# The delta layer's z weights split in two parts, and a gate row of the attention layer made late: one Trainium2 core

## The chip, the cores and the metric

The kernel runs on one core of one Trainium2 chip, as one program that is launched once. The metric is the device time of a run in microseconds (us). Three runs of the kernel before gave 1406.49, 1402.58 and 1404.82, a median of 1404.82; the execution that was profiled took 1404.2, its span on the core, from the first to the last instruction, 1402.4. Engines are called by the profile's names: PE (TensorE, the matmuls), PEld (its weight loads), DVE (VectorE), ACT (ScalarE), POOL (GpSimd), SP (the queue that issues the weight transfers).

## What is computed

Three layers follow each other on one sequence of 256 tokens of width 1024, all in float32. Cut to what matters here:

```
cond = silu(c)
for i in range(2):                                    # i = 0: delta rule, i = 1: forgetting attention
    mod = cond @ ada_w[i] + ada_b[i]                  # 3 x 1024
    shift, scale, gate = split(mod, 3)
    h = rmsnorm(x, norm_w[i]) * (1 + scale) + shift
    y = gdn_mixer(h, ...) if i == 0 else fox_mixer(h, ...)
    x = x + gate * y
x = rmsnorm(x, final_norm_w)

def gdn_mixer(h):   # q, k: 1024, v: 2048, z: 2048 columns of h @ w_in
    o = gated_delta_rule(conv_silu(q, k, v), ...)     # in chunks, by inverses of triangular matrices
    return (rmsnorm(o) * silu(z)) @ w_out
def fox_mixer(h):   # q, k, v, z of h @ w_in, and f, 16 columns
    cum = cumsum(log_sigmoid(f + f_bias))             # decides the logits of every head
    return (attention(q, k, v, cum) * silu(z)) @ w_out
```

The third layer (sliding-window attention, pooling, and 256 gathers of expert rows for each of 16 block-head pairs) isn't touched.

## The kernel before

**Weights.** All weights of the layers stand in a list of units, `plan` (from L271). A unit is 512 KB: 128 partitions by 4 blocks of 256 columns. `load` (L303) issues a unit's transfer on SP into one of 4 buffers named `raw`. `cast` (L311) then makes two tiles of it: `hi` on ACT (L329), the weight rounded to the fp32r format, and `lo` on DVE (L330), what the rounding left; `hi` and `lo` have 4 buffers each. `unit` (L339) hands the next one to PE and casts up to 3 ahead. With the two parts, a product of float32 values is three fp32r matmuls: x's high part by `hi`, x's low part by `hi`, x's high part by `lo`. So a unit makes 24 matmuls of 256 columns (the tile `pd`).

**Whole units.** `whole` (L335) names the units that are not cast: the second half (index 1 of the third number) of every unit of `awi`, the delta layer's input weights. There `raw` itself goes to PE as float32 against the float32 activations `xw`: 8 matmuls, which the profile shows as 16 passes (`pd<-raw,xw` for z, `pd<-xw,raw` for q, k, v). `awi` has column blocks 0 to 7 for q and k, 8 to 15 for v, 16 to 23 for z.

**Modulation.** `ada` (L594) makes one 128-element column of `mod` at a time: a 512 KB transfer of ada_w into a `raw` buffer, and one DVE instruction, the dot product `jk` (L600), that reads it with `silc`, silu of c. There are 48: 16 at the start, the other 32 from a generator `trickle` that `unit` steps once for each unit from the tenth on. Columns 24 to 39 are the attention layer's shift and scale, 40 to 47 its gate. `gate_row` (L631) turns 8 gate columns into a row, `gaterow`, on all partitions: 8 matmuls of 128 columns (`ps<-const,mod`, 16 passes) and 2 ACT copies (L628).

**Order.** The program is written by small tasks (`Mix`, L158) that take turns, and a scheduler then fixes one order for each engine. Each engine's instructions stand and run in that one order. The delta layer's list is `GDN_DENSE` (L48), the attention layer's `FOX_DENSE` (L49): v0 (2 units), q0 and q1 (4 units each, for q and k), v1, z0, and so on. PSUM has 2 buffers `pd`; a finished chunk is copied out of its `pd` by ACT (for q and k: `fd` L1127 and `fsq` L1129, of which `fd` has 2 buffers, given back when PE has transposed them, `ps<-const,fd`).

**The attention layer's start.** `last_dense` (L386) ends the delta layer by token blocks and makes the attention layer's features `fm` (ACT L408, DVE L492, L493). Then `gate_row(1)` is run (L1072). The task `forget` (L1076) makes the forget gate: its weights `bf` are split into `bfh` and `bfl` on DVE, an instruction that is kept behind the last `jk` written so far (L522); PE multiplies (`ps<-fm,bfh`), ACT copies (`bfc`), PE transposes, and DVE computes softplus in a chain of some 28 small instructions (`fx`, `spf`) that ends in `dup` (L569); PE's `ps<-const,dup` sums it up, and ACT and DVE store it as `nrow`, which every head's logits need. `fox_scale` (L1094) normalises q and k on DVE (`fss`, `frs`, `fd`).

Of the kernel before, what the change touches and what calls it, by code (L numbers as in the profile page):

```python
# [210 lines left out]
def build(nc, tc, ctx, I, out, dbg=None, stop=None):  # L211
# [32 lines left out]
    def t4(name, shape=(128, 1024), dt=F32):  # L244
        return t4p.tile(list(shape), dt, name=name, tag="t4", bufs=T4)


    def row_ap(n, w):
        return bass.AP(tensor=I["row"].tensor, offset=I["row"].offset + RO[n], ap=[[0, 128], [1, w]])
# [21 lines left out]
    plan = []  # L271
# [29 lines left out]
    trickle = [iter(())]  # L301
# [32 lines left out]

    def whole(i):  # L335

        return i < len(plan) and plan[i][0] == "awi" and plan[i][2] == 1

    def unit(key, ahead=LA):  # L339
        assert plan[at["use"]] == key, (plan[at["use"]], key)  # L340
# [6 lines left out]
    A2 = (("A", 0, 0, 256, 0), ("A", 1, 0, 256, 256))  # L347
    B2 = (("B", 0, 0, 128, 0), ("B", 0, 128, 128, 256))

    def dense(n, j, items, xf, kgs=(0, 1)):  # L350

        return (yield from dense_all(n, [j], items, xf, kgs))[0]

    def dense_all(n, js, items, xf, kgs=(0, 1)):

        yield from PD.get(len(js))
        pts = [psd.tile([128, 512], F32, name="pd") for _ in js]
        for (ki, kg), (j, pt) in itertools.product(enumerate(kgs), zip(js, pts)):  # L360
            wh, wl_ = unit((n, j, kg))
            for ni, (kind, bi, c0, w, o0) in enumerate(items):
                for k in range(KU):
                    xh, xl, *xw = xf(kg * KU + k)
                    if wl_ is None:
                        xh = xw[0]
                    if kind == "A":
                        ts = slice(bi * 128, bi * 128 + 128)
                        cs = slice(c0, c0 + w)
                        prods = [(xh[:, ts], wh[:, k, cs])]  # L370
                        if wl_ is not None:
                            prods += [(xl[:, ts], wh[:, k, cs]), (xh[:, ts], wl_[:, k, cs])]
                    else:
                        w = T
                        cs = slice(c0, c0 + 128)
                        prods = [(wh[:, k, cs], xh)]
                        if wl_ is not None:
                            prods += [(wh[:, k, cs], xl), (wl_[:, k, cs], xh)]
                    for i, (l, r) in enumerate(prods):
                        mm(pt[:, o0:o0 + w], l, r, start=ki == 0 and ni == 0 and k == 0 and i == 0,  # L380
                           stop=ki == len(kgs) - 1 and ni == len(items) - 1 and k == KU - 1 and i == len(prods) - 1,
                           skip_group_check=True)
                    yield 0
        return pts
# [48 lines left out]
    def run(gen):  # L433

        out = []

        def task():
            out.append((yield from gen))

        M.spawn(0, task())  # L440
        M.run()
        return out[0]


    def ahead(task, n):

        if not n:
            yield from task
            return
        while True:  # L450
            with tc.high_priority(offset=n):
                try:
                    y = next(task)
                except StopIteration:
                    return
            yield y
# [21 lines left out]
    def squares(part, src):  # L478

        jk = act.tile([128, D], BF, name="jka", bufs=1)  # L480
        return A.activation(jk[:, :src.shape[1]], src, AF.Square, accum_out=part).ins
# [112 lines left out]
    def ada(ts):  # L594

        for t in ts:
            w = wts.tile([128, KU * CW], F32, name="raw", bufs=RAW_BUFS)
            nc.sync.dma_start(w, I["ada"][:, t, :])
            jk = act.tile([128, D], BF, name="jk", bufs=1)
            i = V.scalar_tensor_tensor(jk, w, 0.5, silc, op0=OP.mult, op1=OP.mult, accum_out=mod[:, t:t + 1])  # L600
            ada_last.append(i.ins)
            ada_done.add(t)
            yield

    def mod_cols(t, n):
        assert ada_done.issuperset(range(t, t + n))
        V.tensor_tensor(mod[:, t:t + n], mod[:, t:t + n], col("ab", 48)[:, t:t + n], op=OP.add)
        return mod[:, t:t + n]
# [11 lines left out]
    def rows_of(row, m):  # L620

        for hf in range(2):
            yield from PS.get()
            p = pss.tile([128, 512], F32, name="ps")
            for k in range(4):
                o = hf * 4 + k
                mm(p[:, k * 128:(k + 1) * 128], m[:, o:o + 1].to_broadcast([128, 128]), ident, start=True, stop=True)
            A.activation(row[:, hf * 512:hf * 512 + 512], p, AF.Copy)  # L628
            PS.put(HOP)

    def gate_row(i):  # L631
        gb = ear.tile([128, 1024], F32, name="gaterow", bufs=1)
        yield from rows_of(gb, mod_cols(24 * i + 16, 8))
        return gb

    def add_gated(pt, gate, j):

        cs = slice(j * CW, (j + 1) * CW)
        p3 = pt.rearrange("p (b c) -> p b c", b=2)
        t = ear.tile([128, 2, CW], F32, name="gt", bufs=1)  # L640
        V.tensor_tensor(t, p3, gate[:, None, cs].to_broadcast([128, 2, CW]), op=OP.mult)
        V.tensor_tensor(xs[:, :, cs], xs[:, :, cs], t, op=OP.add)

    def add_gated_block(b, jj, pt, gate):
        cs = slice(jj * 512, (jj + 1) * 512)
        t = ear.tile([128, 512], F32, name="gt", bufs=1)
        V.tensor_tensor(t, pt, gate[:, cs], op=OP.mult)
        V.tensor_tensor(xs[:, b, cs], xs[:, b, cs], t, op=OP.add)
        return xs[:, b, cs]
# [61 lines left out]
    def gates():  # L711
        yield 3 * HOP
        pba = yield from small_proj("aba", 32, hx, "aba")
        A.activation(beta, pba[:, :, 0:16], AF.Tanh, scale=0.5)
        V.tensor_scalar(beta, beta, 0.5, 0.5, op0=OP.mult, op1=OP.add)
        ax_ = gp_.tile([128, 32], F32, name="ax")
        V.tensor_tensor(ax_.rearrange("p (b h) -> p b h", b=2), pba[:, :, 16:32],
                        dtb[:, None, :].to_broadcast([128, 2, 16]), op=OP.add)
        PS.put(HOP)
        sp = softplus(ax_, 32, "spa")  # L720
        A.activation(alog, alog, AF.Exp)
        V.scalar_tensor_tensor(g_tm, sp.rearrange("p (b h) -> p b h", b=2), -1.0,
                               alog[:, None, :].to_broadcast([128, 2, 16]), op0=OP.mult, op1=OP.mult)
        yield 4 * HOP
        yield from PS.get()
        pg = pss.tile([128, 3, 16], F32, name="ps")
        mm(pg[:, 0:2], C["tri"], g_tm, start=True, stop=True)
        mm(pg[:, 2], C["cross"], g_tm[:, 0], start=True, stop=True)
        V.tensor_scalar(gsum, pg, -1.0, None, op0=OP.mult)
        PS.put(HOP)  # L730
        grow.append((yield from head_rows(g_tm, C["tri"], C["tri"], "grow")))
        ev_gates.set(HOP)
# [304 lines left out]
        for d in GDN_DENSE[:-1]:  # L1037
            yield from {"q": qk_chunk, "v": v_chunk, "z": z_chunk, "w": w_out}[d[0]](int(d[1]))

    trickle[0] = ada(range(16, 48))  # L1040
    M.spawn(0, ahead(gates(), PR_QK))
    M.spawn(0, ahead(invert(0), PR_INV))
    M.spawn(0, ahead(invert(1), PR_INV))
# [25 lines left out]
    fx = ctx.enter_context(ExitStack())  # L1069
    fp = fx.enter_context(tc.tile_pool(name="fox", bufs=1, side="right", reuse_waits="tile"))  # L1070
    hx = lambda kt, fm=fm: (fm[0][:, kt], fm[1][:, kt])
    gate1 = run(gate_row(1))  # L1072
    nrow = []
    ev_f = Event(M)

# [170 lines left out]
    xo1 = lambda kt: (ohi[:, kt], olo[:, kt])  # L1246
# [4 lines left out]
    lnm = t4("lnm")  # L1251
    nc.scalar.dma_start(lnm, row_ap("lnm", 1024))

    def fox_dense():
        for d in FOX_DENSE:
            yield from {"q": fox_qk, "v": fox_v, "z": fox_z}[d[0]](int(d[1]))
        for i in range(4):
            yield from pdone[i].wait()
        for j in range(4):
            add_gated((yield from dense("bwo", j, A2, xo1, (0,))), gate1, j)  # L1260
            PD.put(HOP)

    M.spawn(-2, ahead(forget(), PR_FS))
    M.spawn(99, fox_dense())
    M.run()
    yb, yl = {}, {}

    def fox_last(b, jj, pt):
        x = add_gated_block(b, jj, pt, gate1)
        squares(ssp[:, b, jj:jj + 1], x)  # L1270
        if jj == 0:
            yb[b] = t4("yb")
        cs = slice(jj * 512, (jj + 1) * 512)
        V.tensor_tensor(yb[b][:, cs], x, fnw[:, cs], op=OP.mult)
        i = squares(ssy[:, b, jj:jj + 1], yb[b][:, cs])
        if jj == 0:
            yl[b] = t4("yl")
        V.tensor_tensor(yl[b][:, cs], yb[b][:, cs], lnm[:, cs], op=OP.mult)
        return i
# [8 lines left out]

    fm = fm_tiles()
    end = last_dense("bwo", 1, xo1, fox_last, blk_rows, fm)  # L1290
    with tc.issue_after(end):
        ss = act.tile([128, 2], F32, name="n_sf")
# [409 lines left out]
```

## Time and profile before

| | |
|---|---|
| median of 3 runs | 1404.82 us (1402.58 to 1406.49) |
| the profiled execution | 1404.2 us, of which 1402.4 are the span |
| PE, PEld busy | 1226.8, 892.3 us |
| DVE, ACT, POOL busy | 1048.0, 571.2, 353.0 us |
| mean granted PE clock | 0.965 of full |
| delta layer | from about 50 to 372 us of the span |
| attention layer | from about 377 to 533 us |
| weight transfers on SP | 512 KB each, median 3.3 to 5.3 us from issue to landing |
| gathers of the last layer | 268.45 MB, from about 740 us to the end |

Busy times overlap. PE's are modelled: a matmul counts from its start to its end, though the next starts long before, so what PE can do is read from the distance of starts. In the chain of waits each piece stands with its start and length. A pass of a float32 matmul counts as one matmul.

### The profile page before, as it was taken

The page shows a single profiled execution, that of the slowest core. Times are in us where ns is not written, and L with a number is a line of the kernel's source. Part 1 is how long each engine was busy: PE and PEld are TensorE (multiplying, and loading weights), DVE is VectorE, ACT ScalarE, POOL GpSimd, SP SyncE. Part 2 cuts the span into 40 slices and gives each one's busy share as a digit, 9 for nine tenths or more (in the row PEclk, how much of TensorE's full clock was granted, in tenths as well). Part 3 has the DMA queues.
Part 4 walks back from the last instruction along what each step waited for, and adds up shares of the span by engine and source line. Part 5 has one row for each costly group of instructions (what it writes and reads, how often), then busy time and mean ns, then how long its engine had stood idle before and what let it go on. Part 6 is the DMA issues. An engine that isn't in the chain of part 4 may idle for free.

```text
span 1402.4 us, 20440 instructions
## 1 busy us (share of the span) xinstructions
PE 1226.8 (87%) x7068; PEld 892.3 (64%) x7068; DVE 1048.0 (75%) x2683; ACT 571.2 (41%) x1310; POOL 353.0 (25%) x295
## 2 busy tenths in 40 slices
PE   2999999999999998999989997878878878777876
PEld 1889988899899988889986753333333323333332
DVE  6799989897777688774788766676767776767655
ACT  3457756574555555564435422122223221222211
POOL 0000000000000000000013436555555455555552
PEclk9999999999999999999999999999999999999999
DMA  8555355533354434335678999999999999999995
GB/s 307 196 185 188 121 182 173 187 119 118 111 183 148 151 117 152 119 107 177 184 278 344 362 376 426 426 425 426 426 426 425 426 425 426 425 426 425 426 425 225
DMA packets 72086, 392.40 MB, mean 280 GB/s; under 512 B 8112, under 2 KB 8624, under 8 KB 39472
## 3 DMA queue, kind: packets, MB, share of 16 engines
q0 software_dynamic: 37296, 268.45, 46.2%
q1 hardware_dynamic: 33104, 117.94, 25.3%
q10 hardware_dynamic: 1584, 4.72, 0.9%
q8 instruction: 56, 0.92, 0.2%
q14 instruction: 46, 0.38, 0.1%
HBM read 390.03 MB, written 1.05 MB: 279 GB/s over the span
## 4 chain that ended last, share of the span: by engine, by line
PE 52%; DMA 34%; DVE 9%; issue 3%; ACT 2%; SPq 0%; POOL 0%; POOLq 0%; DVEq 0%; ACTq 0%
PE pd L218 29%; DMA er<-uv,idx 29%; PE pacc L218 9%; PE ps L218 7%; PE acc L218 2%; PE ip L218 2%; DVE lo L330 2%; PE ps L222 1%; DMA er<-uv,i 1%; DMA raw<-awi 1%; PE po L218 1%; DVE jk L1605 1%; DVE jk L600 1%; PE pt L222 1%; DMA xs<-x 1%
## 5 line engine op out<-in xcount | busy, mean ns | idle before, releaser
L218 PE MATMUL pacc<-er,dg 128*128 128x512 f32 x1024 | 490.4, 634 | 119.0 <-ACT dg L1615 116.1
L1602 POOL DMA_INDIRECT er<-uv,idx x253 | 330.2, 1305 | 743.2 <-DVE xs L1484 435.6
L218 PEld LDWEIGHTS pacc<-er,dg 128*128 128x128 f32 x1024 | 201.0, 202 | 393.3 <-issue 227.8
L1605 DVE SCALAR_TENSOR_TENSOR jk<-er,xn 128x1024 bf16<-128x1024 f32 x256 | 312.7, 1222 | 176.8 <-DMA er<-uv,idx 176.5
L330 DVE TENSOR_TENSOR lo<-raw,hi 128x1024 fp32r<-128x1024 f32 x138 | 168.2, 1222 | 67.6 <-ACT hi L329 67.2
L329 ACT ACTIVATE hi<-raw 128x1024 fp32r<-128x1024 f32 x138 | 146.2, 1060 | 143.3 <-PE pd L218 107.0
L218 PE MATMUL pd<-fm,hi 128*128 128x256 f32 x1008 | 199.9, 295 | 3.3 <-ACT hi L329 3.3
L1609 ACT ACTIVATE ge<-dots,r 128x4 f32<-128x4 f32 (+2 forms) x79 | 23.4, 296 | 415.7 <-DVE jk L1605 415.7
L218 PEld LDWEIGHTS pd<-fm,hi 128*128 128x128 f32 x1008 | 160.2, 193 | 9.1 <-issue 4.1
L218 PE MATMUL pd<-fm,lo 128*128 128x256 f32 x504 | 145.7, 289 | 0.0
L218 PE MATMUL pd<-hi,fm 128*128 128x256 f32 (+1 forms) x608 | 116.9, 290 | 0.6 <-DVE fm L492 0.6
L218 PEld LDWEIGHTS pd<-fm,lo 128*128 128x128 f32 x504 | 96.9, 192 | 1.7 <-issue 1.7
L218 PEld LDWEIGHTS pd<-hi,fm 128*128 128x128 f32 x608 | 95.6, 192 | 1.7 <-PE ps L218 0.8
L1615 ACT ACTIVATE dg<-const,ge 128x128 f32<-128x128 f32 x250 | 81.0, 390 | 38.2 <-DVE ge L1611 32.5
L218 PE MATMUL pd<-lo,fm 128*128 128x256 f32 (+1 forms) x304 | 86.6, 286 | 0.0
L218 PE MATMUL pd<-xw,raw 128*128 128x256 f32 x256 | 67.6, 389 | 2.5 <-DVE xw L508 2.5
L600 DVE SCALAR_TENSOR_TENSOR jk<-raw,silc 128x1024 bf16<-128x1024 f32 x48 | 58.6, 1220 | 2.6 <-DMA raw<-ada 2.2
L823 POOL TENSOR_SCALAR_AFFINE_SELECT am<-am 128x256 f32<-128x256 f32 x16 | 6.5, 406 | 209.5 <-DVE am L821 198.8
L218 PEld LDWEIGHTS pd<-lo,fm 128*128 128x128 f32 x304 | 58.0, 191 | 0.2 <-DVE lo L330 0.2
L869 ACT ACTIVATE is<-acc 128x256 f16<-128x256 f32 x96 | 36.9, 385 | 31.2 <-PE acc L218 29.4
L218 PEld LDWEIGHTS pd<-xw,raw 128*128 128x128 f32 x256 | 44.0, 190 | 6.5 <-DVE xw L508 2.8
L875 DVE TENSOR_TENSOR iy<-ip,fac 128x256 f16<-128x256 f32 x96 | 40.5, 422 | 7.3 <-PE ip L218 5.9
(393 smaller groups left out, 2102.1 us busy)
## 6 DMA issues: line engine op xcount, KB each, us to landing
raw<-ada SPq DMA_DIRECT2D x48, 512.0 KB, 4.3
raw<-awi SPq DMA_DIRECT2D x48, 512.0 KB, 4.1
raw<-bwi SPq DMA_DIRECT2D x32, 512.0 KB, 3.3
raw<-wi SPq DMA_DIRECT2D x30, 512.0 KB, 3.4
raw<-awo SPq DMA_DIRECT2D x16, 512.0 KB, 3.4
raw<-wqy SPq DMA_DIRECT2D x12, 512.0 KB, 5.3
raw<-bwo SPq DMA_DIRECT2D x8, 512.0 KB, 3.7
raw<-wau SPq DMA_DIRECT2D x8, 512.0 KB, 3.6
```

Of the source, the lines that this page charges most:

```text
L218: nc.tensor.matmul(o, l, r, **kw)
L222: nc.tensor.transpose(o, i, e)
L329: A.activation(hi, r3, AF.Copy)
L330: V.tensor_tensor(lo, r3, f(hi), op=OP.subtract)
L600: i = V.scalar_tensor_tensor(jk, w, 0.5, silc, op0=OP.mult, op1=OP.mult, accum_out=mod[:, t:t + 1])
L823: G.affine_select(am, am, pattern=[[0, 2], [1, 128]], base=0, channel_multiplier=-1, compare_op=OP.not_equal, fill=1.0)
L869: A.activation(s[:, 0:2], acc[:, 0:2], AF.Copy)
L875: V.tensor_tensor(y, p, bc2(FH[f"m{m}"]), op=OP.mult)
L1602: G.indirect_dma_start(out=r, out_offset=None, in_=I["uv"], in_offset=bass.IndirectOffsetOnAxis(ap=idx[:, b, h, s + i:s + i + 1], axis=0))
L1605: at["dot"] = V.scalar_tensor_tensor(jk, r[:, 0:D], 1.0, xn[:, b], op0=OP.mult, op1=OP.mult, accum_out=dots[:, i:i + 1]).ins
L1609: A.activation(ge, dots, AF.Gelu, scale=r3[:, b:b + 1])
L1615: A.activation(dg, ident, AF.Copy, scale=ge[:, i:i + 1])
```

## The change

`whole` now also asks that the column block is under 16: z's second halves are cast and multiplied in two parts like the others. The delta layer's `trickle` ends with column 39; columns 40 to 47 are made in the attention layer, one at each of its first 8 units. `gate_row(1)` is run after the last z chunk of the attention layer, ahead of its output weights.

```diff
     def whole(i):
 
-        return i < len(plan) and plan[i][0] == "awi" and plan[i][2] == 1
+        return i < len(plan) and plan[i][0] == "awi" and plan[i][1] < 16 and plan[i][2] == 1
...
-    trickle[0] = ada(range(16, 48))
+    trickle[0] = ada(range(16, 40))
...
     hx = lambda kt, fm=fm: (fm[0][:, kt], fm[1][:, kt])
-    gate1 = run(gate_row(1))
+    trickle[0] = ada(range(40, 48))
...
+    gate1 = []
+
     def fox_dense():
         for d in FOX_DENSE:
             yield from {"q": fox_qk, "v": fox_v, "z": fox_z}[d[0]](int(d[1]))
+        gate1.append((yield from gate_row(1)))
         for i in range(4):
             yield from pdone[i].wait()
         for j in range(4):
-            add_gated((yield from dense("bwo", j, A2, xo1, (0,))), gate1, j)
+            add_gated((yield from dense("bwo", j, A2, xo1, (0,))), gate1[0], j)
             PD.put(HOP)
...
-        x = add_gated_block(b, jj, pt, gate1)
+        x = add_gated_block(b, jj, pt, gate1[0])
```

What moves on the engines, at three places. First DVE before, from the last feature split of the attention layer's start on: `lo` is a unit's second part, `fx` and `spf` the forget gate's chain.

```order
L493 TENSOR_TENSOR fm_4717<-fmv_4929,fm_4717 128x4x128
L330 TENSOR_TENSOR lo_4937<-raw_4726,hi_4936 128x1024
L330 TENSOR_TENSOR lo_4943<-raw_4728,hi_4942 128x1024
L330 TENSOR_TENSOR lo_4987<-raw_4834,hi_4986 128x1024
L330 TENSOR_TENSOR lo_5017<-raw_4940,hi_5016 128x1024
L1080 TENSOR_TENSOR fx_5079<-ps_5076,small_81 128x32
L1083 TENSOR_SCALAR fx_5079<-fx_5079 128x32
```

The chain begins after units 1 to 4, and `bfh` isn't here: it stands far back, in the delta layer. The same stretch of DVE in the changed kernel (`jk` is a modulation column):

```order
L330 TENSOR_TENSOR lo_5272<-raw_5104,hi_5271 128x1024
L600 SCALAR_TENSOR_TENSOR jk_5108,mod_92<-raw_5106,silc_89 128x1024
L330 TENSOR_TENSOR lo_5312<-raw_5138,hi_5311 128x1024
L600 SCALAR_TENSOR_TENSOR jk_5142,mod_92<-raw_5140,silc_89 128x1024
L492 CAST bfh_5154<-bfr_5153 128x128
L1099 TENSOR_REDUCE fss_5418<-fsq_5308 128x8
L493 TENSOR_TENSOR bfl_5155<-bfr_5153,bfh_5154 128x128
L330 TENSOR_TENSOR lo_5352<-raw_5241,hi_5351 128x1024
L600 SCALAR_TENSOR_TENSOR jk_5245,mod_92<-raw_5243,silc_89 128x1024
L1080 TENSOR_TENSOR fx_5201<-ps_5198,small_81 128x32
L600 SCALAR_TENSOR_TENSOR jk_5279,mod_92<-raw_5277,silc_89 128x1024
```

The first row is unit 6, so `bfh` now comes after unit 7 and the second `jk`, and the chain after unit 8 and the third; from `fx` to `dup` there stand 5 more `jk` and 5 `lo`, where before there were 3 `lo`. Then PE at `dup`, in the changed kernel (`pd_5482` is the last chunk of q1, `pd_5561` is v1, `fd_5306` and `fd_5385` are q0's two copies):

```order
L218 MATMUL pd_5482<-lo_5391,fm_4845 128x256
L218 MATMUL ps_5333<-const_79,dup_84 128x128 x2
L222 MATMUL ps_5513<-const_79,fd_5306 128x128 x4
L222 MATMUL ps_5520<-const_79,fd_5385 128x128 x4
L218 MATMUL pd_5561<-hi_5444,fm_4845 128x256 x2
```

`dup` stood after 128 products of this layer (5 units and a part) and now stands after 240, which is all of v0, q0 and q1; of these, 126 stand ahead of the first `bfh` matmul and 135 ahead of the transposes of `bfc`. On SP the eight `ada` transfers stand between the transfers of units 6 and 14, one to one.

## Rows read from the trace of the kernel before

**Rows 1.** The page's first line.

```profile
span 1402.4 us, 20440 instructions
```

**Rows 2.** Busy time by stretch: stretch, length, PE, PEld, DVE, ACT, POOL, clock, DMA.

```profile
60.00:195.00 135.00, 133.07 (x1107) 120.84 (x1105) 124.07 (x333) 85.71 (x218) 6.53 (x16) 1.00 0.51 171
195.00:265.00 70.00, 68.33 (x591) 62.51 (x590) 63.45 (x166) 41.49 (x102) 3.20 (x8) 1.00 0.52 171
...
382.00:402.00 20.00, 19.41 (x159) 18.09 (x158) 15.97 (x42) 10.24 (x19) 0.00 (x0) 1.00 0.58 195
402.00:430.00 28.00, 28.00 (x236) 27.65 (x236) 19.39 (x43) 15.31 (x21) 0.00 (x0) 1.00 0.52 173
```

**Rows 3.** Chain of waits, attention layer: start, length, engine, tile, line, count.

```profile
386.94 4.63 DVE lo L330 x4
...
401.68 0.21 DVE dup L569
401.93 0.71 PE ps L218 x4
...
413.19 0.87 PE ps L222 x8
414.06 11.52 PE pd L218 x96
...
457.37 17.28 PE pd L218 x144
```

**Rows 4.** PE in order of time, delta layer: six float32 passes of z, the next matmul.

```profile
319.80 1.46 PE L218 MATMUL pd<-raw,xw 128*128 128x256 f32 x6
...
321.10 0.61 PE L218 MATMUL ip<-tf,am 128*128 128x128 f32 x4
```

**Rows 5.** The tile zg: when z's eight chunks were copied out.

```profile
L912 ACT ACTIVATE zg<-pd x8: 592/599/632, 79.2 to 333.6; 128x512 f32<-128x512 f32 x8
```

**Rows 6.** All engines in order of time, where the gate row stood.

```profile
379.89 1.14 PE L218 MATMUL ps<-const,mod 128*128 128x128 f32 x8
...
380.92 1.22 DVE L330 TENSOR_TENSOR lo<-raw,hi 128x1024 fp32r<-128x1024 f32 x1
...
381.56 1.50 ACT L408 ACTIVATE fmv<-ps,mod,msc 128x128 f32<-128x128 f32 x4
381.71 1.16 PE L218 MATMUL ps<-const,mod 128*128 128x128 f32 x8 [0.69 <-ACT gaterow L628]
...
382.62 0.36 PE L218 MATMUL pd<-lo,fm 128*128 128x256 f32 x1
```

**Rows 7.** DVE groups, 382 to 430 us: busy, mean ns, idle before.

```profile
L1099 DVE TENSOR_REDUCE fss<-fsq 128x8 f32<-128x512 f32 x4 | 2.7, 680 | 0.0
L1103 DVE TENSOR_TENSOR fd<-fd,frs 128x512 f32<-128x512 f32 x4 | 2.6, 688 | 0.1
```

**Rows 8.** DVE in order of time: a modulation column, bf's split, two steps of the chain.

```profile
263.42 1.22 DVE L600 SCALAR_TENSOR_TENSOR jk<-raw,silc 128x1024 bf16<-128x1024 f32 x1
...
269.79 0.22 DVE L492 CAST bfh<-bfr 128x128 fp32r<-128x128 f32 x1
270.05 0.29 DVE L493 TENSOR_TENSOR bfl<-bfr,bfh 128x128 fp32r<-128x128 f32 x1
...
395.18 0.19 DVE L555 TENSOR_TENSOR spf<-spf 128x32 f32<-128x32 f32 x1
395.41 0.18 DVE L556 TENSOR_SCALAR spf<-spf 128x32 f32<-128x32 f32 x1
```

**Rows 9.** Transfers by line: count, size, median us to landing.

```profile
raw<-ada SPq DMA_DIRECT2D x48, 512.0 KB, 4.3
```

**Rows 10.** Busy time by stretch after PE's wait at the attention layer's end.

```profile
536.00:538.00 2.00, 0.00 (x0) 0.00 (x0) 1.82 (x8) 1.03 (x4) 0.00 (x0) 0.75 0.48 168
538.00:540.00 2.00, 1.63 (x7) 1.63 (x8) 1.75 (x12) 0.00 (x0) 0.00 (x0) 0.50 0.00 0
...
542.00:544.00 2.00, 2.00 (x12) 2.00 (x12) 1.47 (x3) 0.60 (x1) 0.00 (x0) 0.54 0.00 0
```

## The prediction

> **What bounds the kernel now.** I read the busy time by stretch first, then the chain of waits, then single engines in order of time. Three things are to be seen. In the delta layer PE and DVE are both nearly full: from 60 to 195 us PE is busy 133.1 of 135 us and DVE 124.1, from 195 to 265 PE 68.3 of 70 and DVE 63.5 [rows 2]. In the attention layer PE alone is full: its products follow each other every 0.120 us (17.28 us for 144, [rows 3]), and DVE has air, 4.0 us of 20 from 382 to 402 and 8.6 of 28 from 402 to 430 [rows 2]. But at the entry of that layer the chain runs through DVE: four `lo`, then the forget chain to `dup` at 401.68, and PE goes on only behind it [rows 3]. So a microsecond of PE work counts nearly everywhere, and DVE work counts in full where PE has nothing left to do ahead of `dup`. The layers behind wait for x, so a shift there reaches the end.
>
> **z in two parts.** A whole unit is 16 float32 passes; six of them lie between 319.80 and 321.10 [rows 4], 0.217 us each, so 3.47 us. In two parts it is 24 matmuls of 0.120 us, 2.88 us. Eight units save 8 x 0.59 = 4.7 us of PE. The Trainium skill, TensorE: Matmul & The Clock Gate, section "Wait — 56ns, not 53.3ns?", gives a warm matmul of N columns N / 2.4 GHz + 2.5 ns, an estimate of 109 ns for 256; by it the saving would be 6.8 us. The rows, with 120 ns, decide. Each unit adds one ACT `hi` and one `lo`, and a `lo` takes DVE 1.16 us (4.63 for four, [rows 3]). ACT has room (85.7 of 135 us, [rows 2]); its price is nothing while PE has other work between the inverses.
>
> DVE gets its relief elsewhere: z's chunks were copied out from 79 to 334 us [rows 5], so about five of the eight new `lo` fall before 195 us, while the eight `jk` that leave were the last of 32, after 195. Before 195 DVE would be busy 124.1 + 5.8 = 129.9 us in a stretch that PE could do in 135 - 4 x 0.59 = 132.6, 98%. If DVE can't be filled beyond its present 92%, the stretch takes 129.9 / 0.919 = 141.3, 6.3 longer; behind it the freed DVE may give back PE's idle 1.7 us [rows 2]. So the delta layer lies between -4.7 - 1.7 = -6.4 and 6.3 - 1.7 = +4.6. I take **-2.5**, nearer to the gain: matmuls of z wait in line with three units cast ahead, and DVE's total in the layer doesn't change (eight `lo` for eight `jk`). SP's eight `ada` transfers leave the delta layer, where every second buffer was theirs; that can only help.
>
> **The gate row.** Where it stood, PE spent two groups of eight passes on it, from 379.89 and 381.71, but products waited for a `lo` that ended at 382.14 anyway, and went on at 382.62; ACT's next feature copies began at 381.56, behind the first gate copy [rows 6]. Taking it out gives about 0.5 us, counted in the next part. In its new place PE is full: eight passes of 128 columns cost 0.87 us [rows 3] to 1.14 [rows 6], so 1.7 to 2.3 for two groups; I take **+1.8**. Its two ACT copies lie beside the wait for the heads.
>
> **The attention layer's entry.** Eight `jk` of 1.22 us [rows 8] go to DVE, and `bfh`, which was made at 269.79 us [rows 8], is now kept behind the second of them; the chain follows behind the third. I add up DVE in its new order, from the last feature split (386.9 less the 0.5) to the end of `dup`: 13 `lo` 15.1, 8 `jk` 9.8, `bfh` and `bfl` 0.5 [rows 8], two `fss` 1.4 and two `fd` 1.4 [rows 7], 28 chain steps at 0.22 (395.18 to 395.41, [rows 8]) 6.2, and 0.8 for 13 steps of `frs` between them and one sum of `mod`: 35.2 us. The same sum reproduces the kernel before: four `lo` from 386.94, 28 steps, three `lo`, one `fss`, 15.0 us, so 401.9; the trace has 401.89 [rows 3].
>
> DVE also waits. `hi` and `lo` have 4 buffers, so unit 5 can be cast when PE is done with unit 1, and so on. PE begins unit 1 in earnest with its `lo`, at 387.6; it is done with units 1, 2, 3 at about 390.1, 393.0 and 395.8, and one ACT copy later `lo` 5, 6 and 7 begin: DVE idles 0.7, 1.1 and 0.5 us there, and 1.0 before `fx`, which needs PE and ACT once each. 3.2 together; `dup` ends at 386.4 + 35.2 + 3.2 = 424.8.
>
> PE in its new order: 126 products are done at 399.4, just as `bfh` comes; 24 matmuls with `bf` (2.9) and 9 products bring the transposes of `bfc` at 403.5; 105 products (12.6) and it stands at `dup` from 416.3. Nothing else is left to it: the next chunk, v1, needs the `pd` buffer of q1's first chunk; that is copied to a `fd` buffer that comes free when PE has transposed q0, and in PE's order these transposes stand behind `dup`. So PE waits 8.5 us, does `dup` (0.5) and the transposes (0.87, [rows 3]), waits for two ACT copies of 0.6 (a copy of this size, [rows 5]), and starts v1 at 427.2. Before, the 240th product ended at 414.06 + 24 x 0.12 = 416.9 [rows 3]: **+10.3**. PE was full until 533 us and has nothing to catch up with. On ACT `nrow`, the q1 copies and a load of sk, which takes silc's buffer and so waits for the last `jk`, are queued in that order; all are done by then, or wait for the same `dup`. Least: no idle DVE, 3.2 less, +7.1. Most: some three of the eight `jk` find their transfer, 4.3 us [rows 9], 1 us late, since two streams now share four buffers: +13.3.
>
> **The clock.** At the attention layer's end PE stood still for some 5 us, and the granted clock then showed half, the lower of its two levels, from 537 to 544 us, 5.4 of it with PE at work [rows 10]. After a wait of 8.5 us I expect the same: between 0 and half of 5.4, 2.7; I take **+2.0**.
>
> **Sum**, from the profiled execution's 1404.2 (span 1402.4, [rows 1], and 1.8 around it): -2.5 + 1.8 + 10.3 + 2.0 = +11.6, 1415.8. It lies 0.6 under the median of the runs, so 1416. The ends: -6.4 + 1.7 + 7.1 + 0 = +2.4, and 4.6 + 2.3 + 13.3 + 2.7 = +22.9, so 1407 and 1427.
>
> **Rivals.** *DVE's air takes it all (faster).* DVE idled 12.6 us from 382 to 430 [rows 2], more than the 9.8 of the `jk`; if `dup` came by 416.3, PE would run through. Then -6.4 - 0.5 + 1.8 = -5.1, about 1399.5. It decides by whether DVE's work from 386.4 to `dup` is under 29.9 us; I count 35.2, and the idle time before lay mostly behind `dup`, where this can't use it. For it speaks the average, against it the order. 0.08.
>
> *DVE is the bound of the delta layer's first half.* The stall as forecast and +4.6 in place of -2.5: about 1423. For it: 98% of DVE in a stretch where it now has 92. Against: the same total over the layer. 0.13.
>
> *Late modulation transfers.* +13.3 in the entry: about 1419. The landing of 4.3 us [rows 9] stands against some 4.7 us and more that each has from the release of its buffer to its turn. 0.08.
>
> *A small loss.* The delta layer gains its full 6.4, the entry costs 7.1 and the clock nothing: 1407. 0.13.
>
> **How the numbers follow.** The forecast has 0.58. What a measurement of this kernel can tell from no change is 0.3%, 4.2 us: faster ends at 1400.6, slower begins at 1409.0. Faster is the first rival, 0.08; within are the small loss and a little of the forecast's low side, 0.14; slower the rest, 0.78. The range from 1405 to 1424 takes in the forecast, both dear cases and the small loss; outside are the first rival and the far ends, under 2 in 10.
>
> **What would show it.** Right: PE stands still once for 7 to 11 us, some 40 us into the attention layer, released by `dup` on DVE, the clock at half behind it; `bfh` comes some 130 us later than before; the delta layer ends 0 to 6 us earlier; `ps<-const,mod` appears shortly before the output weights without a wait. Wrong: a `dup` that PE doesn't wait for, or a delta layer whose end moves by more than 6 us either way, which would mean that its own order, not the attention layer's entry, makes the time.

## The result and the profile after

The changed kernel takes 1417.42 us (median of 6 runs, 1415.22 to 1418.19), the kernel before beside it 1402.23 (6 runs). The ratio is 1.0097, with a 95% interval from 1.0086 to 1.0107: 13.6 us slower by that ratio (the medians differ by 15.2). Forecast were 1416 and slower. The page's first lines of the changed kernel, whose profiled execution took 1418.18 us:

```profile
span 1416.4 us, 20613 instructions
...
PE 1226.7 (87%) x7132; PEld 895.5 (63%) x7132; DVE 1053.2 (74%) x2691; ACT 579.8 (41%) x1318; POOL 358.4 (25%) x295
```

The span is 14.0 us longer than [rows 1], PE's busy time the same to 0.1 us (1226.8 before): PE doesn't do more, it waits more. To see where, I cut the span at three marks that both kernels have: PE's first `ps<-g_tm` (the delta layer's gates), its first `ps<-dgr` (the attention layer's features) and the start of its last `pd<-lo,omh` (the end of the attention layer's output products).

| us | to the gates | delta layer | attention layer | rest |
|---|---|---|---|---|
| before | 65.7 | 307.6 | 159.9 | 869.2 |
| changed | 65.9 | 306.9 | 172.7 | 870.8 |

The attention layer makes 12.8 of the 14.0. Its entry in the chain of waits (start, length, engine, tile, line, count):

```profile
385.20 4.54 DVE lo L330 x4
...
397.37 1.23 DVE jk L600 x2
398.59 0.03 DVE bfh L492
398.62 5.37 DMA raw<-ada
...
407.03 4.51 DMA raw<-ada
...
422.89 0.21 DVE dup L569
...
423.15 1.22 PE ps L218 x4
424.37 0.87 PE ps L222 x4
...
425.26 0.60 ACT fd L1127
425.86 0.50 ACT fsq L1129
...
426.40 8.91 PE pd L218 x72
```

It answers to [rows 3]: four `lo`, the forget chain, `dup`. But `bfh` comes at 398.6, in place of 269.79 [rows 8], transfers of modulation columns stand in the chain, and `dup` comes 21.2 us later than before. PE in order of time shows what it does meanwhile (in brackets: idle before, and who ended it). First PE at `dup` in the kernel before:

```profile
401.93 0.71 PE L218 MATMUL ps<-const,dup 128*128 128x128 f32 x4 [0.59 <-DVE dup L569]
```

and in the changed kernel:

```profile
413.79 0.28 PE L218 MATMUL pd<-lo,fm 128*128 128x256 f32 x1
...
415.59 0.28 PE L218 MATMUL pd<-lo,fm 128*128 128x256 f32 x1
423.15 1.22 PE L218 MATMUL ps<-const,dup 128*128 128x128 f32 x4 [7.28 <-DVE dup L569]
424.16 1.91 PE L222 MATMUL ps<-const,fd 128*128 128x128 f32 x8
426.40 0.51 PE L218 MATMUL pd<-hi,fm 128*128 128x256 f32 x2 [0.32 <-ACT fsq L1129]
...
514.33 1.06 PE L218 MATMUL ps<-const,mod 128*128 128x128 f32 x8
...
518.96 1.11 PE L218 MATMUL ps<-const,mod 128*128 128x128 f32 x8
```

The wait at `dup` is 7.28 us, as forecast, where it was 0.59; v1 begins at 426.40. In the kernel before, the 240 products that stand ahead of v1 were done, by [rows 3], at 416.9. From the layer's first mark to v1 it is 53.6 us, in place of 43.5: 10.1 of the layer's 12.8 are lost up to there. The gate row's 16 passes stand at 514 and 519, with no wait in front of them. The busy time by stretch (stretch, length, PE, PEld, DVE, ACT, POOL, clock, DMA), first the kernel before from 265 us on, which [rows 2] doesn't have:

```profile
265.00:345.00 80.00, 79.30 (x674) 73.06 (x673) 66.63 (x180) 48.51 (x117) 3.16 (x8) 1.00 0.38 126
```

and the changed kernel:

```profile
60.00:195.00 135.00, 127.42 (x1109) 117.55 (x1108) 123.15 (x316) 89.13 (x218) 7.73 (x16) 1.00 0.52 172
195.00:265.00 70.00, 68.53 (x632) 64.49 (x630) 64.05 (x176) 44.56 (x113) 3.16 (x8) 1.00 0.40 130
265.00:345.00 80.00, 79.82 (x695) 74.84 (x695) 64.08 (x165) 49.25 (x116) 3.20 (x8) 1.00 0.32 100
...
418.00:420.00 2.00, 0.00 (x0) 0.00 (x0) 2.00 (x12) 0.37 (x1) 0.00 (x0) 0.91 0.72 227
420.00:422.00 2.00, 0.00 (x0) 0.00 (x0) 2.00 (x6) 0.00 (x0) 0.00 (x0) 0.50 0.77 244
...
424.00:426.00 2.00, 2.00 (x10) 1.67 (x9) 0.42 (x1) 1.12 (x3) 0.00 (x0) 0.50 0.91 303
426.00:428.00 2.00, 1.68 (x14) 1.60 (x14) 0.69 (x1) 2.00 (x5) 0.00 (x0) 0.89 0.75 258
```

In the delta layer PE stands idle 7.6 us of the first 135, where it was 1.9 [rows 2]. From 60 to 345 us its idle time grows from 4.3 to 9.2, which takes back the 4.7 us that z in two parts saves. While DVE works its way to `dup` it is busy 2.00 of 2.00 us, and the granted clock falls to half inside the wait, to come back as v1 begins.

### The profile page after: what moved, and what is told of

The parts are those of the page before. It is cut to its first block, busy times and chain, and to the rows that moved or that the text cites. A ratio compares the mean times of both kernels' runs of the same rounds, so it can differ in the third digit from the quotient of the medians.

```text
span 1416.4 us, 20613 instructions
## 1 busy us (share of the span) xinstructions
PE 1226.7 (87%) x7132; PEld 895.5 (63%) x7132; DVE 1053.2 (74%) x2691; ACT 579.8 (41%) x1318; POOL 358.4 (25%) x295
## 4 chain that ended last, share of the span: by engine, by line
PE 45%; DMA 38%; DVE 11%; issue 3%; ACT 3%; SPq 0%; POOL 0%; POOLq 0%; ACTq 0%; DVEq 0%
DMA er<-uv,idx 31%; PE pd L218 25%; PE pacc L218 7%; PE ps L218 6%; DMA raw<-awi 3%; DVE lo L330 2%; PE acc L218 2%; PE ip L218 1%; DVE jk L600 1%; DMA raw<-ada 1%; DVE jk L1608 1%; ACT hi L329 1%; DMA er<-uv,i 1%; PE ps L222 1%; PE po L218 1%
## 5 line engine op out<-in xcount | busy, mean ns | idle before, releaser
L1605 POOL DMA_INDIRECT er<-uv,idx x253 | 334.5, 1322 | 756.9 <-DVE xs L1487 451.4
L1608 DVE SCALAR_TENSOR_TENSOR jk<-er,xn 128x1024 bf16<-128x1024 f32 x256 | 312.5, 1221 | 177.9 <-DMA er<-uv,idx 176.7
L330 DVE TENSOR_TENSOR lo<-raw,hi 128x1024 fp32r<-128x1024 f32 x146 | 177.9, 1221 | 71.1 <-ACT hi L329 70.7
L329 ACT ACTIVATE hi<-raw 128x1024 fp32r<-128x1024 f32 x146 | 154.7, 1060 | 157.2 <-PE pd L218 109.0
L218 PE MATMUL pd<-hi,fm 128*128 128x256 f32 (+1 forms) x736 | 141.2, 290 | 1.6 <-DVE fm L492 1.3
L218 PEld LDWEIGHTS pd<-hi,fm 128*128 128x128 f32 x736 | 116.8, 194 | 3.1 <-issue 1.8
L218 PE MATMUL pd<-lo,fm 128*128 128x256 f32 (+1 forms) x368 | 105.5, 288 | 2.9 <-DVE lo L330 2.9
L218 PEld LDWEIGHTS pd<-lo,fm 128*128 128x128 f32 x368 | 70.8, 193 | 3.5 <-DVE lo L330 3.4
```

Of the source, the lines that this page charges most:

```text
L218: nc.tensor.matmul(o, l, r, **kw)
L329: A.activation(hi, r3, AF.Copy)
L330: V.tensor_tensor(lo, r3, f(hi), op=OP.subtract)
L1605: G.indirect_dma_start(out=r, out_offset=None, in_=I["uv"], in_offset=bass.IndirectOffsetOnAxis(ap=idx[:, b, h, s + i:s + i + 1], axis=0))
L1608: at["dot"] = V.scalar_tensor_tensor(jk, r[:, 0:D], 1.0, xn[:, b], op0=OP.mult, op1=OP.mult, accum_out=dots[:, i:i + 1]).ins
```

## The experiments

The theory: the loss is made at the attention layer's entry, by the eight `jk` and the late `bfh` ahead of `dup`; the late gate row adds some 2 us; z in two parts is worth nothing, since DVE gives back what PE saves. The rivals: z's new `lo` make the loss; the place of `bfh` alone makes it; the columns' transfers make it, not DVE's time. Each kernel was timed beside the kernel before; "against before" is worked out from the ratio's interval. The stage lengths are each run's profiled execution's, cut at the same marks (rest of the span not shown):

| run | ratio (95%) | against before, us | delta layer | attention layer |
|---|---|---|---|---|
| changed kernel | 1.0097 (1.0086 to 1.0107) | +13.6 | 306.9 | 172.7 |
| 1 z alone | 1.0026 (1.0014 to 1.0037) | +3.7 | 312.3 | 159.0 |
| 2 modulation alone | 1.0087 (1.0068 to 1.0106) | +12.2 | 307.4 | 174.5 |
| 3 `bfh` early | 1.0060 (1.0042 to 1.0079) | +8.4 | 309.8 | 167.1 |
| 4 columns after q1 | 1.0039 (1.0024 to 1.0054) | +5.5 | 307.0 | 166.5 |
| 5 delta's columns later | 1.0110 (1.0091 to 1.0128) | +15.4 | 308.0 | 172.5 |
| 6 both later | 1.0044 (1.0029 to 1.0060) | +6.2 | 305.5 | 165.7 |
| 7 gate row alone | 1.0022 (1.0010 to 1.0034) | +3.1 | 308.2 | 161.2 |
| 8 other units in parts | 0.9994 (0.9982 to 1.0007) | -0.8 | 308.0 | 158.9 |
| 9 z, columns much later | 1.0056 (1.0035 to 1.0077) | +7.9 | 312.5 | 159.6 |
| 10 `bfh` late alone | 1.0012 (0.9999 to 1.0026) | +1.7 | 307.8 | 161.4 |
| 11 columns spaced | 1.0060 (1.0043 to 1.0077) | +8.4 | 307.5 | 168.6 |
| 12 short `jk` | 1.0044 (1.0029 to 1.0060) | +6.2 | 306.0 | 165.1 |

Stage lengths repeat well where the instructions are the same: the attention layer as before has 158.9 to 159.9 (before, 1, 8, 9; mean 159.4), the delta layer as before 307.6 to 308.2 (before, 7, 10; mean 307.9). The rest, the same instructions in all, goes from 866.5 to 871.4. So a microsecond is read from the stages, not from the sum. Cut once more at v1 (the layer's 241st product), the attention layer falls into an entry of 42.5 to 43.5 us (before, 1, 8, 9; mean 42.9) and a stretch behind it that has 116.7 in all four.

**1. z alone.**

```diff
--- the kernel before
-        return i < len(plan) and plan[i][0] == "awi" and plan[i][2] == 1
+        return i < len(plan) and plan[i][0] == "awi" and plan[i][1] < 16 and plan[i][2] == 1
```

> The kernel before with one part of the change alone: z's weight units in two parts; gate row and modulation stay where they were. Theory (the loss is made at the attention layer's entry, and the delta layer alone is worth what the changed kernel's trace showed at its end, -0.5 us): within 0.3% of before, -0.5 us, at most -3, since here the eight jk stay in the delta layer and DVE gets eight lo more there. Rival (z's second part pays in full): -4.7 us. Rival (DVE becomes the bound of the delta layer): 5 us or more slower, most of it before 195 us. No wait of PE at dup in either.

+3.7 us, all in the delta layer (312.3 against 307.9) and no trace of it in the attention layer; a miss for all three figures, nearest to the rival in which DVE is the bound. Busy time by stretch in this run:

```profile
60.00:195.00 135.00, 126.23 (x1087) 116.25 (x1087) 122.07 (x315) 87.83 (x213) 7.78 (x16) 1.00 0.52 172
195.00:265.00 70.00, 65.37 (x605) 60.99 (x604) 64.31 (x175) 43.38 (x111) 3.29 (x8) 1.00 0.46 151
265.00:345.00 80.00, 79.30 (x694) 73.92 (x692) 68.31 (x169) 50.24 (x119) 4.14 (x8) 1.00 0.41 136
```

PE idles 8.8 + 4.6 + 0.7 = 14.1 us, 9.8 more than before; less the 4.7 saved that is +5.1, close to the +4.4 measured. DVE is no busier than before in the first stretch (122.1 against 124.1), though it has more to do per unit. The waits of PE from 60 to 265 us (who waited for whom, total, times, longest):

```profile
PE acc L218 <- DVE iy L875: 2.6, 4, 1.3
PE ip L218 <- ACT is L869: 2.5, 4, 0.9
PE ps L218 <- ACT dt L804: 2.1, 2, 1.6
PE acc L218 <- ACT tt L899: 1.8, 2, 1.1
```

They are short waits in the chains of the triangular inverses, on DVE and on ACT, which got eight `hi` of its own. In the first stretch more of them are for ACT (6.5 us) than for DVE (2.1), and in the changed kernel too (4.4 and 3.0). ACT itself stood at `hi`, from 60 to 195 us, for weights that hadn't landed (total, times, longest), before, in this run and in the changed kernel:

```profile
ACT hi L329 <- DMA raw<-awi: 5.3, 6, 1.8
ACT hi L329 <- DMA raw<-awi: 15.8, 11, 2.8
ACT hi L329 <- DMA raw<-awi: 14.1, 10, 2.8
```

So late weight transfers, whose `raw` buffers the columns share, are a rival to DVE's load here. Which of them makes PE's waits wasn't tried apart.

**2. Modulation alone.**

```diff
--- the changed kernel
-        return i < len(plan) and plan[i][0] == "awi" and plan[i][1] < 16 and plan[i][2] == 1
+        return i < len(plan) and plan[i][0] == "awi" and plan[i][2] == 1
```

> The changed kernel with z's second halves whole again: only the gate's modulation and its row are moved. Theory (the entry makes the loss): as slow as the changed kernel within 2 us, so +12 to +15 against before, or a little less, with bfh at about 398 us and a wait of PE at dup of 7 to 8 us. Rival (z in two parts makes the loss, DVE bound of the delta layer): within 3 us of before.

+12.2: the loss is here, in an attention layer of 174.5, with `bfh` at 400.7 and a wait of 6.99 us at `dup`. The rival falls. The delta layer, eight `jk` shorter, gains only 0.5 (307.4): they stood behind 195 us, where PE had only 2.4 us of idle time to lose. Together with run 1, z in two parts costs 4.4 us beside 32 `jk`, and 306.9 - 307.4 = -0.5 beside 24; and the eight `jk` cost 0.5 without z's `lo`, but 312.3 - 306.9 = 5.4 beside them.

**3, 10, 12. What delays `dup`.** Run 3 takes `bfh` back into the delta layer and leaves the `jk`; run 10 has the late `bfh` without any `jk`; run 12 leaves place and transfers, and takes DVE's time away (it leaves out seven eighths of each of the eight dot products).

```diff
--- run 3, from the changed kernel
-        with tc.issue_after(ada_last[-1]):
+        with tc.issue_after(ada_last[min(len(ada_last), 40) - 1]):
--- run 10, from the kernel before
-            V.tensor_tensor(lo, r3, f(hi), op=OP.subtract)
+            lo_last.append(V.tensor_tensor(lo, r3, f(hi), op=OP.subtract).ins)
...
-        with tc.issue_after(ada_last[-1]):
+        with tc.issue_after((lo_last if name == "bf" else ada_last)[-1]):
...
-        yield 3 * HOP
+        u0 = at["use"]
+        while at["use"] < u0 + 5:
+            yield HOP
--- run 12, from the changed kernel
-            i = V.scalar_tensor_tensor(jk, w, 0.5, silc, op0=OP.mult, op1=OP.mult, accum_out=mod[:, t:t + 1])
+            n = 128 if t >= 40 else D
+            i = V.scalar_tensor_tensor(jk[:, :n], w[:, :n], 0.5, silc[:, :n], op0=OP.mult, op1=OP.mult, accum_out=mod[:, t:t + 1])
```

> The changed kernel, with bf's split kept behind the delta layer's last modulation column instead of the attention layer's second: bfh goes back to the delta layer, while the eight jk stay in the attention layer; five or six of them still stand ahead of dup. Theory (the place of bfh and the eight jk both delay dup): some 5 us of the wait at dup go, so the time is +6 to +9 against before. Rival A (the place of bfh alone): no wait of PE at dup, +2 to +3 against before. Rival B (the jk and their transfers alone): as slow as the changed kernel, +13 to +15.

> The kernel before with bf's split alone moved: behind the seventh lo of the attention layer, where the changed kernel has it, without any jk beside it. PE's order has dup behind 195 products of the layer, not 128 and not 240. Theory (the wait at dup is made by the jk on DVE and their transfers together with the late bfh, not by bfh's place alone): the sum of DVE's work up to dup is ten lo, two fss, bf's split, 28 steps and a few of frs, 22 us and 3 of waits, so dup at about 411 us, just as PE comes to it: a wait under 2 us, 0 to +2 against before. Rival (the place of bfh alone makes most of the loss): a wait at dup of 5 us or more, +5 or more.

> The changed kernel, with the eight gate columns' jk over 128 elements instead of 1024; it leaves out seven eighths of these dot products, while the eight transfers of 512 KB stay. The order that results has dup behind 201 products. Theory (DVE's time for the jk is what delays dup, 9.8 us of 35): some 5 us less DVE work ahead of dup, the wait there falls to under 3 us, +5 to +8 against before. Rival (the transfers, which take the raw buffers of the weights, make the delay): the wait at dup stays at 6 us or more, +11 to +14.

PE at `dup`, in order of time, in run 3:

```profile
413.55 0.71 PE L218 MATMUL ps<-const,dup 128*128 128x128 f32 x4 [2.32 <-DVE dup L569]
421.86 1.26 PE L222 MATMUL ps<-const,fd 128*128 128x128 f32 x8 [1.54 <-DVE fd L1103]
```

in run 10:

```profile
410.31 0.71 PE L218 MATMUL ps<-const,dup 128*128 128x128 f32 x4 [0.53 <-DVE dup L570]
```

and in run 12:

```profile
410.09 0.71 PE L218 MATMUL ps<-const,dup 128*128 128x128 f32 x4 [1.41 <-DVE dup L569]
```

All three came as the theory expected. In run 3 the wait at `dup` falls from 7.28 to 2.32 us, with 1.54 more behind it, for `fd`. In run 10 the place of `bfh` alone costs 2.0 us of the layer (161.4 against 159.4): its rival falls. These 2.0 are not at `dup`, where the wait is 0.53 and was 0.59 before; they are a wait of PE for a `lo`, at a place where the kernel before had the products with `bf` to do (385.95 to 388.2 us):

```profile
386.07 0.39 PE L218 MATMUL pd<-lo,fm 128*128 128x256 f32 x1 [2.10 <-DVE lo L331]
```

Beside the `jk` the same place costs 172.7 - 167.1 = 5.6. Without the `jk`'s DVE time, the transfers still there, the layer is 7.6 us shorter (165.1) and the wait falls from 7.28 to 1.41: the transfers' rival falls too, for this place. (The scheduler's order differs too: `dup` stands behind 202 products of the layer in run 3, 195 in run 10 and 201 in run 12, not 240. In run 12 that is 39 products less on PE, 4.7 us, and three `lo` and two `fd` less on DVE, 4.7 us as well: for the wait at `dup` the two cancel. How much of the layer's length is order and how much DVE's time can't be told apart.) The theory holds for the wait: DVE's time in front of `dup` makes it, and a late `bfh` costs more beside the `jk` (5.6) than without them (2.0).

**4 and 11. The columns behind q1.**

```diff
--- run 4, from the changed kernel
-    trickle[0] = ada(range(40, 48))
...
-        for d in FOX_DENSE:
+        for n, d in enumerate(FOX_DENSE):
+            if n == 3:
+                trickle[0] = ada(range(40, 48))
--- run 11, from run 4
+    def spaced(steps):
+        for _ in steps:
+            yield
+            yield
...
-                trickle[0] = ada(range(40, 48))
+                trickle[0] = spaced(ada(range(40, 48)))
```

> The changed kernel, with the eight gate columns started only behind v0, q0 and q1: z in two parts and the late gate row stay, but no jk stands ahead of dup and bfh is back in the delta layer. Theory: the wait at dup is gone with all that hangs on it; what is left is the late gate row, +1.8 us, and the delta layer, -0.5 us: +1 to +2 us against before, within 0.3%. Rival (the loss belongs to the late gate row or to DVE's load in the attention layer as a whole, wherever the columns stand): +8 us or more.

> The run with the gate's columns behind v0, q0 and q1 (+5.5 against before), with the columns at every second unit instead of every one. Theory (what is left there, beside the late gate row, is the columns' transfers and jk standing in front of lo, DMA raw<-ada 2.7% of the layer's chain): half the load at a time, so the waits of PE between 430 and 520 us, 4.1 there, fall below 2, and the time comes to +3, which is the late gate row. Rival (the columns cost the same wherever they stand in this layer): +5 to +6.

Both missed. In run 4 the wait at `dup` is back to 0.59, what it was, but the layer has 166.5: gate row 1.8 (run 7), and 5.3 more. Spacing made it worse, 168.6. From 430 to 520 us PE's waits are 3.4 us in run 4 (not the 4.1 that the expectation of run 11 says) and 5.3 in run 11. The DVE groups show why. Run 4, from 425 to 470 us (busy, mean ns, idle before and what ended it):

```profile
L600 DVE SCALAR_TENSOR_TENSOR jk<-raw,silc 128x1024 bf16<-128x1024 f32 x7 | 8.6, 1224 | 4.7 <-DMA raw<-ada 4.7
```

and run 11, from 425 to 482:

```profile
L600 DVE SCALAR_TENSOR_TENSOR jk<-raw,silc 128x1024 bf16<-128x1024 f32 x8 | 9.8, 1223 | 9.3 <-DMA raw<-ada 9.3
```

Here DVE stands still at a `jk` until its transfer lands, 4.7 and 9.3 us in total, and what stands behind the `jk` waits with it: in run 11's chain of waits a column's transfer is followed by `fd`, and that by PE.

```profile
475.78 4.68 DMA raw<-ada
...
481.72 0.61 DVE fd L1108
482.38 1.26 PE ps L222 x8
```

In the changed kernel, from 382 to 430 us, the same groups are

```profile
L330 DVE TENSOR_TENSOR lo<-raw,hi 128x1024 fp32r<-128x1024 f32 x13 | 15.6, 1221 | 3.1 <-ACT hi L329 3.1
L600 DVE SCALAR_TENSOR_TENSOR jk<-raw,silc 128x1024 bf16<-128x1024 f32 x8 | 9.7, 1213 | 1.8 <-DMA raw<-ada 1.8
```

So the columns cost at each of the places tried in this layer: ahead of `dup` mainly by DVE's time, behind it by the wait for their transfers as well. How the scheduler came to place the spaced columns ahead of their data wasn't tried.

**5, 6 and 9. The delta layer's columns later.**

```diff
--- run 5, from the changed kernel, and run 6, from run 4
-TRICKLE = 9
+TRICKLE = 17
--- run 9, from run 1
-TRICKLE = 9
+TRICKLE = 25
```

> The changed kernel, with the delta layer's modulation columns started eight units later, so that z's first lo have fewer jk beside them on DVE. The attention layer is as in the changed kernel. Theory (z in two parts gains nothing because DVE is full before 200 us, where PE's waits grew from 3.8 to 8.7 us between 100 and 200): those waits shrink, 2 to 4 us faster than the changed kernel, +9 to +12 against before. Rival (the waits come from the order of PE's work, not from DVE's load): as slow as the changed kernel, +13 to +15. The wait at dup stays at 7 to 8 us in both.

> The changed kernel with both moves: the delta layer's columns eight units later, the gate's columns behind v0, q0 and q1. Theory: the run with the second move alone came to +5 against before; the first takes 2 to 4 us off, so +1 to +3, and no wait at dup. Rival (the delta layer does not care): +5.

> z's units in two parts, all 32 modulation columns in the delta layer, gate row as before, but the columns start 16 units later, so that they end shortly before the layer does: DVE is relieved before 250 us and loaded from 265 to 345, where it was busy 66.6 of 80 us. Theory (in the delta layer PE's waits follow DVE's load from stretch to stretch, and a column costs nothing only where DVE has air): the waits before 265 us shrink and some come up behind it; between the kernel before and the run with z alone (+3.7): 0 to +3. If it is faster than before by over 2 us, z in two parts is worth its place with late columns. Rival (z's lo cost in any place): +4 or more.

No gain in any: +15.4, +6.2, +7.9. (The expectation of run 5 has PE's waits from 100 to 200 us as 3.8 and 8.7; by the busy times PE idles 1.5 us there before and 6.1 in the changed kernel.) Of the delta layer's lengths one is longer than with the early columns (308.0 against 306.9) and one shorter (305.5 against 307.0). The waits moved, though, as the busy times of run 5 show:

```profile
60.00:195.00 135.00, 133.41 (x1164) 123.11 (x1163) 119.50 (x311) 91.02 (x223) 6.52 (x16) 1.00 0.45 146
195.00:265.00 70.00, 65.15 (x573) 59.88 (x572) 62.57 (x169) 40.63 (x103) 3.22 (x8) 0.98 0.46 151
```

and those of run 9:

```profile
265.00:345.00 80.00, 77.04 (x672) 71.72 (x670) 74.60 (x174) 48.09 (x112) 3.91 (x8) 1.00 0.56 188
345.00:370.00 25.00, 20.05 (x159) 18.71 (x158) 24.06 (x64) 6.69 (x8) 0.00 (x0) 1.00 0.80 271
```

Relieved, the first stretch keeps PE at 133.4 of 135 us even with z in two parts; then PE idles 4.9 of 70 us in run 5, and in run 9 5.0 of 25 where DVE is at 24.06. The waits follow the `jk`, but not DVE's time alone: the columns' transfers move with them, and ACT's wait for late weights in the first stretch falls from 14.1 us to 6.8 in run 5 and 6.1 in run 9. The theory's place for the waits holds, its size doesn't, and its cause, DVE's load, isn't shown: moving the columns about gives nothing.

**7. Gate row alone.**

```diff
--- run 7, from the changed kernel
-        return i < len(plan) and plan[i][0] == "awi" and plan[i][1] < 16 and plan[i][2] == 1
+        return i < len(plan) and plan[i][0] == "awi" and plan[i][2] == 1
...
-    trickle[0] = ada(range(16, 40))
+    trickle[0] = ada(range(16, 48))
...
-    trickle[0] = ada(range(40, 48))
```

> The kernel before with one part of the change alone: the gate row behind the attention layer's last z chunk; all modulation columns stay in the delta layer, z as before. Theory: its 16 passes, which lay in a wait of PE at the layer's entry, now stand in a full PE: +1.8 us, at most +2.5, within 0.3%. Rival (where the row stands costs nothing, the run with late columns lost its +5 through the columns): 0. Second rival (the row holds up the output weights' products behind it): +3 or more, with PE's time from the last head's product to the end of the layer about 3 us longer.

+3.1 (1.4 to 4.8), and in the attention layer 161.2 against 159.4, +1.8. The middle of the measured interval lies over the +2.5 that was given as the most, and the time alone can't exclude the second rival. Cut at v1, the layer has 42.1 and 119.3: where the row stands now it costs 2.6 (119.3 against 116.7), and where it stood 0.8 are gained (42.1 against 42.9). Of the 2.6 its two groups of passes make 1.9, by the distance of starts.

**8. Other units in two parts.**

```diff
--- the kernel before
-        return i < len(plan) and plan[i][0] == "awi" and plan[i][2] == 1
+        return i < len(plan) and plan[i][0] == "awi" and plan[i][2] == 1 and plan[i][1] not in (12, 13, 14, 15, 22, 23)
```

> The kernel before, with other second halves in two parts: not z's eight, but the six of v2, v3 and z3, which PE takes from about 265 us on, where DVE is busy 66.6 of 80 us and has no jk left after 300. Theory (a unit in two parts is worth 0.59 us where DVE has air and costs time where it is full): 6 x 0.59 = 3.5 us less PE work, at most that; 1 to 3.5 us faster than before, within 0.3%. Rival (a unit in two parts gains nothing anywhere): 0 or slower.

-0.8 (-2.5 to +1.0), a delta layer of 308.0: the rival. The 3.5 us that PE saves don't show, also where DVE had air; from 60 to 370 us PE's idle time is 2.0 us more, the rest isn't found.

No version is measurably faster than the kernel before; runs 8 and 10 can't be told from it.

## Why the prediction was right

**The attention layer's entry, +10.3.** Right in kind and size: +10.1 up to v1. From the last feature split to the end of `dup` 38.4 us were forecast; the trace has 385.2 to 423.1, 37.9. PE was forecast at `dup` from 416.3 and v1 at 427.2; measured 415.9 and 426.4. The parts, by the runs: DVE's time for the `jk`, with the order that it brings, 7.6; what is left without it, 165.1 - 159.4 = 5.7, holds the gate row's 1.8, and the place of `bfh`, 2.0 by itself. That leaves 1.9 without a run that shows it. That the sum came so near is in part luck, for two errors in it cancel. DVE's waits were put at 3.2; it waited 3.1 for ACT's `hi`, 1.0 before `fx` and 1.8 for the columns' transfers, which the forecast kept for its dear case: 5.9. The work was put at 35.2 and was 32.0, most of the difference in the chain: its 28 steps were put at 0.22 us each, the distance at which they follow each other alone, but now `lo`, `jk` and `frs` stand between them, and from 414.03 to 415.46 us fourteen small instructions start, one each 0.1 us.

**The gate row, +1.8.** Mis-sized. That run 7's layer is 1.8 longer agrees by chance: the forecast's 1.8 was the price in the new place, which is 2.6 in run 7, and 2.7 in the changed kernel (119.4 behind v1, against 116.7); the gain where it stood was counted in the entry.

**The clock, +2.0.** Mis-sized. I looked for it in the products behind the wait; but the clock came back at 426.5, as v1 began. What it cost lies in the work released by `dup`: its four matmuls took 1.22 us against 0.71 [rows 3], and from `dup`'s end to v1 it was 3.3 us (423.1 to 426.4) where the forecast had 2.4 (424.8 to 427.2). So at most +0.9, and inside the entry's 426.4; behind v1 the changed kernel is as long as run 7 (119.4 and 119.3). The clock was at half from 382.1 to 385.5 us as well, but behind that PE came to a wait for a `lo` (0.80 us, to 386.38) all the same.

**z in two parts, -2.5.** Mis-sized: -0.7 in the profile. The step that failed is "I take -2.5, nearer to the gain: ... DVE's total in the layer doesn't change". The total hides where the load stands: PE's idle time before 195 us grew by 5.7, with five of the new `lo` there and one `jk` less, while what the eight `jk` leave free lies later, where PE had little idle time to lose. The second rival's waits came at its place, though not at its price: they gave back the gain and no more. Its cause, DVE as the bound, isn't shown: DVE was no busier there than before (123.2 against 124.1). A term put at nothing failed beside it, "ACT has room ...; its price is nothing": PE's waits for ACT before 195 us grew from 1.2 to 4.4 us, more than those for DVE (0.4 to 3.0), and ACT stood 14.1 us at `hi` for late weights. Whether these transfers or DVE's load make the waits stays open. The products themselves took 0.120 us also after the change (15 from 413.79 to 415.59). The Trainium skill, TensorE: Matmul & The Clock Gate, section "Wait — 56ns, not 53.3ns?", gives an estimate of 109 ns; the trace doesn't agree, and the 6.8 us by that figure would have been further off.

**The sum.** Forecast +11.6, the profiled executions differ by 14.0: entry, row and clock 14.1 forecast, 12.8 measured; delta layer -2.5 and -0.7; +0.2 ahead of it and +1.6 behind, which lies within the spread of the rest (866.5 to 871.4). So the total has two errors that cancel, about 1.3 and 1.8 us; that it came this near is luck, that it is slower, and by the entry, is not.

## What to carry to other kernels

Before work is moved from a full engine to one with average air, write down that engine's order up to the instruction that others wait for, and add up what now stands ahead of it: here that sum, 38 us, was right in kind (to half a microsecond, with two errors of some 3 us that cancel), and the average said the opposite. A microsecond that an engine saves counts only if the others, and the transfers that they wait for in their order, keep up in the same stretch; compare stretch by stretch, not layer totals. An operand's split that is tied to "the last instruction so far" moves with whatever is added there.

## What the runs showed that I had not expected

The clock in run 3: with the same delta layer as the changed kernel, its granted clock was 0.71 from 184 to 188 us and 0.50 from 188 to 192, behind a stretch in which none of PE's waits was over 0.7 us, and this delta layer took 309.8 us where the others with these instructions took 306.0 to 307.5. So the half clock came here without a long wait. The layer was 2.3 to 3.8 us longer; that the clock makes all of it isn't shown:

```profile
180.00:184.00 4.00, 2.68 (x30) 2.09 (x29) 3.15 (x9) 3.19 (x10) 0.00 (x0) 1.00 0.57 215
184.00:188.00 4.00, 2.59 (x21) 2.13 (x20) 2.84 (x8) 3.62 (x10) 0.00 (x0) 0.71 0.41 131
188.00:192.00 4.00, 4.00 (x26) 3.67 (x25) 2.53 (x8) 1.97 (x6) 0.00 (x0) 0.50 0.00 0
```
